# A bitwise top-k threshold search: its per-bit comparison on GpSimd instead of VectorE, and a larger background share

## Chip, cores, metric

One core of a Trainium2 chip. The metric is the device time of one execution in microseconds (us); the median of three runs is given. PE is TensorE's matmul, PEld its weight load, DVE is VectorE, ACT is ScalarE, POOL is GpSimd, SP is the queue that issues most DMAs.

## What is computed

One layer of an encoder on x of 2048 tokens by 1024 channels, float32. A projection gives queries, a latent key and value, indexer queries and keys, pool inputs and gates. An indexer scores every admissible key for each query; the 256 best keys are kept, and 8 heads attend to these alone. A pooling mixer and two sigmoid gates, an output projection, a layer norm and a convolutional feed-forward follow. Of the reference, only this bears on the change:

```python
idx_score = jnp.einsum('bqh,bqhs->bqs', wib.astype(jnp.float32) * head_w_scale, rel)
idx_score = jnp.where(admissible[None], idx_score, -jnp.inf)
_, sel = lax.top_k(idx_score, topk)
```

## The kernel before

The tokens are cut into 16 blocks of 128 queries, and four groups of four blocks. The main stream of work is, in order: projection of the indexer columns (`proj_index`, four groups); then for each group the pool columns, the queries and the gates (`proj_pool`, `proj_q`, `proj_gates`); then attention over 32 units (a unit is one group and one head), the mixing of the branches (`mix_out`), and the feed-forward. Every matmul is three float32r matmuls on split operands, and the main stream is written so that TensorE always has the next one.

The top-k is found without sorting. For each query, `index_scores` builds the scores, and `select` builds a threshold F bit by bit, from bit 31 down to 0. In each bit, a block's scores are counted against the candidate in F in two pieces: ACT sums the signs of one piece into `ca`, and DVE counts the other piece into `cd`. The blocks go in three background jobs (`GROUPS`): blocks 2 to 7, 8 to 11 and 12 to 15 (blocks 0 and 1 need no selection). Each job has two halves of two to four blocks that take turns, so that one half's counts lie beside the other half's decision. `decide` is that decision: is 2 cd - ca below a limit, and so which candidate is next. There are 32 bits, 3 jobs and 2 halves, so 192 decisions. At the end of a job each block is finished: counts against the found threshold, signs (`sg`), a mask of equals, a running count along the row (`tensor_tensor_scan`, one DVE instruction of up to 2048 elements), and the mask `m`, stored to DRAM.

What sets the order of the work: the selection is a Python generator in the list `bg`. `turn` (L461 and after) runs after every step of the main stream. It adds `RATE` times the modelled TensorE time to a credit (at most `CAP`, 1.5 us), and pulls background steps while the credit is positive and the modelled backlog of DVE and ACT is under 3 us. A step costs the larger of its modelled DVE and ACT time (`Paced` has the model; POOL's time isn't charged). So `RATE` and the cost of a step set how far the selection has come at any point of the main stream.

The other thing that pulls the generator is `load_mask` (L1191 and after). It is called in the attention when a block's mask is to be loaded, and if that block isn't finished yet, it runs the rest of the job at once:

```python
while self.selected < b:
    if next(self.bg[0][1], "end") == "end":
        self.bg.pop(0)
```

All engine instructions are recorded by a wrapper (`Paced`, L133), so the trace names that line for all; tiles tell them apart. `g`, `h` and `F` are the tiles of a decision, `cd` and `ca` its two sums, `mx` a score tile's row extreme in the attention. Each engine runs its instructions in the order in which they stand.

Of the kernel before, what the change touches and what calls it, by code (L numbers as in the profile page):

```python
# [15 lines left out]
OP = mybir.AluOpType  # L16
# [52 lines left out]
FINE = "fine"  # L69
PAUSE = "pause"  # L70
GRAIN = 1
RATE = 0.75
CAP = 1.5
EARLY = 2
SWITCH = "A--"
# [270 lines left out]
class Kern:  # L346
# [83 lines left out]
    def turn(self, step=None):  # L430
# [8 lines left out]
        pe, work = self.clocks.pe, self.clocks.work  # L439
        self.credit = min(self.credit + RATE * (pe - self.seen), CAP)  # L440
        self.seen = pe
# [632 lines left out]
    def select(self, halves):  # L1074
# [6 lines left out]
        nc = self.nc  # L1081
# [13 lines left out]
        def decide(k, bit):  # L1095
            cd, ca = acc[k]
            nh = len(halves[k])
            g_ = self.sml([P, 4], tag="g")[:, :nh]
            h = self.sml([P, 4], I32, tag="h")[:, :nh]
            f2 = self.sml([P, 4], I32, tag="F")[:, :nh]  # L1100
            lim = 2.0 * TOPK - 1.0 - ws[k]
            nc.vector.scalar_tensor_tensor(g_, cd, 2.0, ca, op0=OP.mult, op1=OP.subtract)
            yield
            if bit == 31:
                nc.vector.tensor_scalar(h, g_, lim, -1.0, op0=OP.is_lt, op1=OP.mult)
                yield
                nc.vector.tensor_scalar(f2, h, 0x40000000, None, op0=OP.bitwise_xor)
            else:
                nc.vector.tensor_scalar(h, g_, lim, float(2 ** bit), op0=OP.is_lt, op1=OP.mult)
                yield  # L1110
                nc.vector.scalar_tensor_tensor(f2, h, 2 ** (bit - 1) if bit else 0, F[k],
                                               op0=OP.bitwise_xor, op1=OP.bitwise_xor)
            F[k] = f2

        pend = None
        for bit in range(31, -1, -1):
            for k, half in enumerate(halves):
                f = F[k].bitcast(F32)
                w, nh = ws[k], len(half)
                cd, ca = self.sml([P, 4], tag="cd")[:, :nh], self.sml([P, 4], tag="ca")[:, :nh]  # L1120
                for i, b in enumerate(half):
                    ja, jd = self.M([P, 1024], BF16), self.M([P, 1024], BF16)
                    nc.scalar.activation(ja[:, :w], back[b], AF.Sign, bias=f[:, i:i + 1], scale=-1.0,
                                         accum_out=ca[:, i:i + 1])
                    n = front[b].shape[1]
                    nc.vector.tensor_scalar(jd[:, :n], front[b], f[:, i:i + 1], None, op0=OP.is_ge, op1=OP.add,
                                            accum_out=cd[:, i:i + 1])
                    if pend:
                        next(pend, None)
                    yield  # L1130
                if pend:
                    for _ in pend:
                        pass
                acc[k] = (cd, ca)
                pend = decide(k, bit)
        for _ in pend:
            pass
        for k, half in enumerate(halves):
# [21 lines left out]
            for i, b in enumerate(half):  # L1160
# [9 lines left out]
                                               op0=OP.mult, op1=OP.subtract)  # L1170
# [953 lines left out]
```

## Time and profile before

| | |
|---|---|
| three runs | 3159.14, 3161.13, 3167.12 us (median 3161.13) |
| the profiled execution | 3160.95 us; span from first to last instruction 3159.2 us |
| mean granted TensorE clock | 0.989 of full speed |
| PE busy | 3041.4 us (96%) |
| PEld busy | 2536.1 us (80%) |
| DVE busy | 2445.5 us (77%) |
| ACT busy | 1613.7 us (51%) |
| POOL busy | 541.5 us (17%) |

How to read it: an engine that is busy for 96% of the span leaves 118 us in which it waits. A change to work on other engines can at most give back such waits, and what a lower granted clock adds around them; the place of each wait in time says which work it hangs on. A busy DVE or ACT costs nothing by itself.

### The profile page before, as it was taken

To read this page: it belongs to the slowest core of one execution; us is meant where nothing else is said; L and a number is where in the kernel's file an instruction comes from. 1 tells how busy PE (TensorE), PEld (TensorE's weight loads), DVE (VectorE), ACT (ScalarE), POOL (GpSimd) and SP (SyncE) were. 2 spreads that over 40 slices of the span, in tenths; PEclk is the share of its full clock that TensorE was granted. 3 is DMA by queue.
4 is the path that set the end of the run, shared out by engine and by line. 5 is a ranking of instruction groups with operands and counts; after the bars stand their busy time and mean duration, and the time that the engine had idled before them with its cause. 6 is when DMAs were issued, how large, how long until landed. Compare 5 with 4: busy or idle time off the path is not lost. (4 is left out here: it accounts for less than half of the span.)

```text
span 3159.2 us, 43928 instructions
## 1 busy us (share of the span) xinstructions
PE 3041.4 (96%) x14750; PEld 2536.1 (80%) x14750; DVE 2445.5 (77%) x4563; ACT 1613.7 (51%) x3085; POOL 541.5 (17%) x528
## 2 busy tenths in 40 slices
PE   8999899999999999979999999999999999999998
PEld 8887688888888788768787778887778888888887
DVE  5588887987699899888776688999886655656676
ACT  3468846874578787657611144444442222433253
POOL 2002010010020221100231234554411111100011
PEclk9999899999999999989999999999999999999999
DMA  7668783755466332221264778887888866998753
GB/s 255 242 208 298 262 336 138 275 213 184 145 256 250 102 104 84 70 80 62 82 225 162 262 259 303 299 296 284 289 305 321 313 214 224 366 397 328 262 199 110
DMA packets 325872, 715.88 MB, mean 227 GB/s; under 512 B 27466, under 2 KB 132366, under 8 KB 325646
## 3 DMA queue, kind: packets, MB, share of 16 engines
q1 hardware_dynamic: 317006, 697.34, 62.0%
q10 hardware_dynamic: 8640, 15.73, 1.3%
q8 instruction: 117, 1.92, 0.3%
q14 instruction: 109, 0.89, 0.1%
HBM read 454.85 MB, written 258.11 MB: 226 GB/s over the span
## 5 line engine op out<-in xcount | busy, mean ns | idle before, releaser
L133 PE MATMUL p<-b,b 128*128 128x512 f32 (+3 forms) x12568 | 2824.0, 381 | 71.3 <-DVE b L133 25.9
L133 PEld LDWEIGHTS p<-b,b 128*128 128x128 f32 x12568 | 2255.5, 190 | 511.0 <-DVE b L133 32.9
L133 DVE TENSOR_TENSOR b<-p,b 128x512 f32<-128x512 f32 (+3 forms) x622 | 390.6, 654 | 144.6 <-PE p L133 97.8
L133 ACT ACTIVATE b<-p 128x512 fp32r<-128x512 f32 (+11 forms) x634 | 360.6, 604 | 259.1 <-PE p L133 244.0
L133 ACT ACTIVATE b<-b 128x512 fp32r<-128x512 f32 (+3 forms) x344 | 270.5, 805 | 323.2 <-DVE b L133 143.4
L133 DVE TENSOR_TENSOR b<-b,b 128x1024 fp32r<-128x1024 f32 (+6 forms) x302 | 340.0, 1136 | 87.5 <-ACT b L133 38.0
L133 ACT ACTIVATE m<-b,F 128x448 bf16<-128x448 f32 (+3 forms) x448 | 366.2, 820 | 52.8 <-DVE F L133 40.3
L133 DVE TENSOR_SCALAR_CACHE_REDUCE m<-b,F 128x512 bf16<-128x512 f32 (+6 forms) x476 | 372.5, 808 | 7.3 <-DMA gm<-m 3.8
L133 ACT ACTIVATE b<-m 128x512 fp32r<-128x512 f32 x215 | 133.3, 628 | 345.0 <-DVE m L133 133.7
L133 DVE SCALAR_TENSOR_TENSOR b<-b,cw,b 128x1023 f32<-128x1023 f32 (+1 forms) x176 | 246.2, 1411 | 69.7 <-ACT b L133 68.7
L133 ACT ACTIVATE b<-b,cw 128x1024 f32<-128x1024 f32 x88 | 106.9, 1236 | 269.5 <-DVE b L133 260.5
L133 POOL TENSOR_TENSOR b<-b,b 128x1024 f32<-128x1024 f32 (+3 forms) x62 | 148.8, 2402 | 490.2 <-DVE b L133 289.4
L133 PE MATMUL p<-ident,b 128*128 128x128 f32 x1248 | 199.0, 278 | 17.0 <-DVE b L133 8.9
L133 ACT ACTIVATE b<-b,mx 128x1024 f32<-128x1024 f32 (+2 forms) x192 | 171.6, 896 | 70.5 <-DVE mx L133 68.1
L133 PEld LDWEIGHTS p<-ident,b 128*128 128x128 f32 x1248 | 154.3, 142 | 53.1 <-DVE b L133 13.1
L133 DVE TENSOR_TENSOR b<-m,b 128x512 fp32r<-128x512 f32 x215 | 155.6, 732 | 53.1 <-ACT b L133 52.9
L133 DVE SCALAR_TENSOR_TENSOR b<-b,ws,b 128x768 f32<-128x768 f32 (+5 forms) x154 | 154.0, 1025 | 42.2 <-ACT b L133 39.3
L133 DVE CUSTOM_DVE_ANT_0 b<-p,b 128x1024 f32<-128x1024 f32 (+7 forms) x128 | 125.6, 984 | 39.1 <-PE p L133 30.9
L133 PE MATMUL p<-kst,b 128*128 128x384 f32 (+3 forms) x656 | 147.8, 358 | 2.8 <-ACT b L133 2.0
L133 ACT ACTIVATE m<-p 128x512 f32<-128x512 f32 (+2 forms) x172 | 100.8, 586 | 74.6 <-PE p L133 67.9
L133 PEld LDWEIGHTS p<-kst,b 128*128 128x128 f32 x656 | 111.0, 188 | 23.1 <-ACT b L133 12.4
L133 DVE TENSOR_TENSOR b<-p,m 128x512 f32<-128x512 f32 x132 | 89.7, 682 | 10.8 <-PE p L133 10.7
(126 smaller groups left out, 1528.4 us busy)
## 6 DMA issues: line engine op xcount, KB each, us to landing
b<-wk SPq DMA_DIRECT2D x339, 512.0 KB
wk<-b SPq DMA_DIRECT2D x211, 512.0 KB
b<-h SPq DMA_DIRECT2D x88, 512.0 KB
b<-in_w_ffn_up_dram SPq DMA_DIRECT2D x44, 512.0 KB
h<-b SPq DMA_DIRECT2D x44, 512.0 KB
b<-vv SPq DMA_DIRECT2D x80, 256.0 KB
hs<-b SPq DMA_DIRECT2D x33, 512.0 KB
b<-hs SPq DMA_DIRECT2D x33, 512.0 KB
```

The costliest lines, as they stand in the source:

```text
L133: return f(*args, **kw)
```

## The change

```diff
-RATE = 0.75
+RATE = 0.8
...
-            nc.vector.scalar_tensor_tensor(g_, cd, 2.0, ca, op0=OP.mult, op1=OP.subtract)
+            nc.gpsimd.tensor_scalar(g_, cd, 2.0, -lim, op0=OP.mult, op1=OP.add)
+            nc.gpsimd.tensor_tensor(g_, g_, ca, op=OP.subtract)
+            nc.gpsimd.tensor_scalar(h, g_, 0.0, float(2 ** bit) if bit < 31 else -1.0, op0=OP.is_lt, op1=OP.mult)
             yield
             if bit == 31:
-                nc.vector.tensor_scalar(h, g_, lim, -1.0, op0=OP.is_lt, op1=OP.mult)
-                yield
                 nc.vector.tensor_scalar(f2, h, 0x40000000, None, op0=OP.bitwise_xor)
             else:
-                nc.vector.tensor_scalar(h, g_, lim, float(2 ** bit), op0=OP.is_lt, op1=OP.mult)
-                yield
                 nc.vector.scalar_tensor_tensor(f2, h, 2 ** (bit - 1) if bit else 0, F[k],
                                                op0=OP.bitwise_xor, op1=OP.bitwise_xor)
```

The comparison of a decision, two DVE instructions (g and h), becomes three POOL instructions on the same small tiles. The next candidate F stays on DVE. A decision is emitted in two pieces instead of three. The rate at which the background gets credit goes from 0.75 to 0.80.

What this moves is seen in the order of the built programs (rows as listed; a long scan along a row prints as SCALAR_TENSOR_TENSOR there, and the attention's score reductions as ISA).

First place, DVE in the third job (blocks 12 to 15), late in its bits. Before, two halves' counts and one decision:

```order
L133 TENSOR_SCALAR m_11324,cd_11321<-b_10000,F_11283 128x896
L133 TENSOR_SCALAR m_11338,cd_11321<-b_10235,F_11283 128x1024
L133 TENSOR_SCALAR m_11352,cd_11349<-b_9546,F_11329 128x768
L133 SCALAR_TENSOR_TENSOR g_11355<-cd_11321,ca_11322 128x2
L133 TENSOR_SCALAR h_11356<-g_11355 128x2
L133 SCALAR_TENSOR_TENSOR F_11357<-h_11356,F_11283 128x2
```

The same kind of place on DVE after the change:

```order
L133 TENSOR_SCALAR m_11155,cd_11152<-b_9964,F_11128 128x896
L133 SCALAR_TENSOR_TENSOR F_11160<-h_11159,F_11090 128x2
L133 TENSOR_SCALAR m_11172,cd_11152<-b_10199,F_11128 128x1024
L133 SCALAR_TENSOR_TENSOR F_11196<-h_11195,F_11128 128x2
L133 TENSOR_SCALAR m_11191,cd_11188<-b_9537,F_11160 128x768
```

And on POOL, the two decisions whose F stand in the fence above:

```order
L133 TENSOR_SCALAR g_11158<-cd_11120 128x2
L133 TENSOR_TENSOR g_11158<-g_11158,ca_11121 128x2
L133 TENSOR_SCALAR h_11159<-g_11158 128x2
L133 TENSOR_SCALAR g_11194<-cd_11152 128x2
L133 TENSOR_TENSOR g_11194<-g_11194,ca_11153 128x2
L133 TENSOR_SCALAR h_11195<-g_11194 128x2
```

DVE loses g and h. F now stands behind one count of the other half (F_11160) or, as F_11196 does, directly behind the last count of its own half, and takes h from POOL.

Second place, DVE in the attention, the finishing of block 14 (tiles of 1920 elements). Before, it stands as one run:

```order
L133 TENSOR_SCALAR b_16109<-b_16108 128x1920
L133 TENSOR_TENSOR m_16175<-p_4852_15930,m_16176 64x512
L133 SCALAR_TENSOR_TENSOR b_16110<-b_16109 128x1920
L133 SCALAR_TENSOR_TENSOR nd_16115<-b_16110,fx_16094,cg_16093 128x1
L133 TENSOR_SCALAR nd_16115<-nd_16115 128x1
L133 TENSOR_SCALAR b_16109<-b_16110,nd_16115 128x1920
L133 TENSOR_TENSOR b_16108<-b_16108,b_16109 128x1920
L133 TENSOR_SCALAR b_16120<-b_16108 128x1920
```

After the change, the same instructions begin as follows:

```order
L133 TENSOR_SCALAR b_14800<-b_14799 128x1920
L133 SCALAR_TENSOR_TENSOR b_14801<-b_14800 128x1920
L133 TENSOR_TENSOR b_14847<-p_4533_14842,b_14847 128x512
L133 SCALAR_TENSOR_TENSOR nd_14839<-b_14801,fx_14785,cg_14784 128x1
L133 TENSOR_TENSOR b_14857<-p_4535_14852,b_14857 128x512
L133 TENSOR_SCALAR nd_14839<-nd_14839 128x1
L133 ISA b_14866,mx_14827<-p_4537_14862,b_14584,mx_14827 128x256
```

Block 14's scan now stands ahead of the place where block 12's stood, with the attention's own work between its steps; block 15's (2048 elements) stands shortly behind that place, and block 13's at the start of the attention. Block 12 is finished before the attention, between the last gates. The whole job has ended when the first of the masks 12 to 15 is asked for, so the loop in `load_mask` finds nothing left to run; in the program before, it ran the remainder of block 14 (its second half's counts among it) and all of block 15.

## Rows read from the trace of the kernel before

**Rows 1.** Windows: from:to, length; busy us (count) by engine; clock, DMA share, GB/s.

```profile
1300.00:1400.00 100.00, 75.71 (x389) 62.59 (x389) 81.70 (x150) 56.01 (x110) 10.12 (x13) 0.86 0.24 80
```

**Rows 2.** Timeline of PE, 1300 to 1400 us: start, us, instruction, [idle before, releaser].

```profile
1321.49 0.44 PE L133 MATMUL p<-ident,b 128*128 128x128 f32 x2 [2.75 <-DVE b L133]
...
1324.65 3.25 PE L133 MATMUL p<-b,b 128*128 128x384 f32 x7 [1.13 <-ACT b L133]
...
1350.11 2.19 PE L133 MATMUL p<-b,b 128*128 128x512 f32 x6 [4.16 <-DVE mx L133]
...
1357.77 0.66 PE L133 MATMUL p<-ident,b 128*128 128x128 f32 x4 [1.45 <-DVE m L133]
1366.06 5.82 PE L133 MATMUL p<-b,b 128*128 128x512 f32 x14 [7.63 <-DVE mx L133]
...
1380.97 2.93 PE L133 MATMUL p<-b,b 128*128 128x512 f32 x6 [7.06 <-DVE mx L133]
```

**Rows 3.** Timeline of DVE, 1340 to 1400 us.

```profile
1357.64 4.14 DVE L133 TENSOR_TENSOR_SCAN b<-b 128x1920 f16<-128x1920 f16 x1
...
1364.78 1.22 DVE L133 CUSTOM_DVE_ANT_0 b<-p,b 128x1024 f32<-128x1024 f32 x1
...
1372.13 4.42 DVE L133 TENSOR_TENSOR_SCAN b<-b 128x2048 f16<-128x2048 f16 x1
```

**Rows 4.** Windows of 10 us around the last two blocks and the two before.

```profile
1260.00:1270.00 10.00, 6.73 (x37) 5.37 (x37) 9.72 (x18) 3.54 (x8) 5.75 (x4) 0.95 0.21 63
1270.00:1280.00 10.00, 10.00 (x56) 8.83 (x56) 8.56 (x17) 8.05 (x20) 0.00 (x0) 0.88 0.00 0
...
1320.00:1330.00 10.00, 7.26 (x27) 5.72 (x28) 8.11 (x20) 4.98 (x12) 2.28 (x2) 0.68 0.00 0
...
1350.00:1360.00 10.00, 6.87 (x33) 5.76 (x33) 5.49 (x10) 6.30 (x11) 2.13 (x2) 0.83 0.00 0
1360.00:1370.00 10.00, 3.94 (x9) 3.14 (x10) 8.57 (x13) 1.83 (x3) 0.00 (x0) 0.56 0.26 86
1370.00:1380.00 10.00, 3.90 (x19) 3.00 (x17) 8.39 (x8) 3.05 (x6) 0.00 (x0) 0.84 0.04 14
1380.00:1390.00 10.00, 9.03 (x39) 7.42 (x40) 7.61 (x14) 4.72 (x8) 1.42 (x2) 0.74 0.69 228
```

**Rows 5.** Timeline of all engines, 1258 to 1272 us, block 12.

```profile
1263.46 4.00 DVE L133 TENSOR_TENSOR_SCAN b<-b 128x1664 f16<-128x1664 f16 x1
1264.06 4.45 POOL L133 TENSOR_TENSOR b<-m,b 128x512 fp32r<-128x512 f32 x1
...
1267.95 0.66 PE L133 MATMUL p<-ident,b 128*128 128x128 f32 x4 [3.13 <-DVE b L133]
```

**Rows 6.** Tiles g and F on DVE: count, duration ns min/median/max, first and last start.

```profile
L133 DVE SCALAR_TENSOR_TENSOR g<-cd,ca x192: 89/157/864, 187.0 to 1213.0; 128x2 f32<-128x2 f32 x160, 128x4 f32<-128x4 f32 x32
L133 DVE TENSOR_SCALAR h<-g x192: 151/169/898, 187.1 to 1222.1; 128x2 int32<-128x2 f32 x160, 128x4 int32<-128x4 f32 x32
...
L133 DVE TENSOR_SCALAR_CACHE_REDUCE m<-b,F x476: 332/868/1283, 186.0 to 1346.0; 128x128 bf16<-128x128 f32 x33, 128x320 bf16<-128x320 f32 x33, 128x768 bf16<-128x768 f32 x23, 128x640 bf16<-128x640 f32 x23
```

**Rows 7.** Timeline of POOL in the branch mixing: small operations of 128x1.

```profile
1627.71 1.31 POOL L133 TENSOR_SCALAR lv<-mv 128x1 f32<-128x1 f32 x1 [2.25 <-DVE mv L133]
...
1629.76 0.19 POOL L133 TENSOR_TENSOR lt<-lr 128x1 f32<-128x1 f32 x1
1630.03 0.19 POOL L133 TENSOR_TENSOR lt<-lt,lv 128x1 f32<-128x1 f32 x1
```

**Rows 8.** Windows: the stretch of the index scores and gates, and the projections after.

```profile
190.00:420.00 230.00, 209.98 (x945) 171.71 (x946) 195.83 (x698) 182.06 (x480) 19.25 (x29) 0.96 0.83 291
420.00:1060.00 640.00, 637.54 (x2914) 528.46 (x2912) 540.53 (x1225) 422.58 (x755) 50.72 (x71) 1.00 0.58 209
```

**Rows 9.** Timeline of PE, 180 to 420 us: its two longest waits there.

```profile
331.49 1.65 PE L133 MATMUL p<-b,wpool 128*128 128x512 f32 x3 [7.34 <-ACT m L133]
336.73 1.65 PE L133 MATMUL p<-b,wpool 128*128 128x512 f32 x3 [3.59 <-ACT m L133]
```

## Prediction

> **What bounds the kernel now.** I read the windows first, to find where TensorE waits at all; then its waits in the one stretch that stood out; then the engine that they name. From 420 to 1060 us, the projections under which most of the selection runs, PE is busy 637.5 of 640 us at full clock [rows 8]: there, work taken off DVE or put on POOL is worth nothing as long as PE goes on being fed. The stretch that stands out is 1300 to 1400 us: PE busy 75.7 of 100, granted clock 0.86 [rows 1]. Its six waits add up to 24.2 us, and the long ones name DVE's `mx`, a score reduction that came late [rows 2]. DVE isn't idle then. From 1357.64 it runs the finishing of block 14, and the next score reduction starts only at 1364.78; block 15's scan follows at 1372.13 [rows 3]. This is the forced run: the masks of blocks 14 and 15 were asked for before their job had ended, `load_mask` pulled the rest of it into DVE's queue in one piece, and the attention's reductions stood behind it. The reader should see two things: the kernel is bound by PE, and the selection costs time only where its steps stand ahead of something that PE needs at once.
>
> **What the waits cost.** A wait costs its own time and a lower granted clock beside it. For the second I take, in a 10 us window, PE's busy time times what the clock lacks [rows 4]. The forced run: waits of 4.16, 1.45, 7.63 and 7.06, together 20.3; clock from 1350 to 1390, 1.2 + 1.7 + 0.6 + 2.3 = 5.9; total 26.2 us [rows 2, 4]. Block 13's scan, which came as an ordinary step: waits of 2.75 and 1.13, clock 2.3 in 1320 to 1330; total 6.2 [rows 2, 4]. Block 12's, also ordinary: one wait of 3.13 behind a scan of 4.00 [rows 5], clock 0.3 + 1.2 [rows 4]; total 4.7. Together 37.0 us hang on the finishing of these four blocks.
>
> **The rate and the cheaper decision.** Both put the selection ahead of where it was: 6.7% more credit per us of TensorE, and two DVE operations fewer in each decision's cost. The order shows the result: the job has ended before mask 12 is asked for, so the forced run goes, and all 37.0 us go with their places. What comes back: block 15's scan stands about where block 12's did and gets its price, 4.7. Block 14's stands somewhat earlier, in the same kind of work; between 4.7 and 6.2, I take 5.4. Block 13's now stands at the start of the attention, among short score tiles; nothing there shows a scan, so it lies between 0 and 6.2, and I take 4.7, the price of the nearest row. Block 12 is finished between the last gates, where PE has whole products in hand, as it had when PE lost 2.5 us in 640 [rows 8]; between 0 and 4.7, I take 2. That is 16.8 us back, and 20.2 gained.
>
> **The decision on POOL.** 192 decisions lose g (157 ns) and h (169 ns) on DVE [rows 6]: 62.6 us of DVE time, at no point the path itself. They gain three POOL operations. Small dependent ones start 0.27 us apart and take 0.19 [rows 7], so 0.27 + 0.27 + 0.19 = 0.73 from the sums to h; the crossings from DVE to POOL and back aren't in these rows, and I give them one more step: 1.0 us as an estimate. POOL has room: 576 times 0.19 is 109 us more, in 870 us of which it used 70 [rows 8]. What matters is who waits. F stands in DVE's queue, and all of DVE waits with it: the splits of the next weights, the other half's counts, and through F also ACT's counts, with the gates' evictions queued behind them. What stands on DVE between a half's last count and its F is the cover. By the order, 42 of the 192 have nothing there, 41 under 0.5 us, and 109 more than that, mostly one count of the other half (0.33 to 1.28 us, median 0.87 [rows 6]). With 1.0 us each, the uncovered rest adds up to 82 us, against 62.6 saved: DVE gets later by some 19 us between 190 and 1060, where it has 133.7 us idle [rows 8]. So this lies beside other work almost everywhere. The exception is 190 to 420, where DVE is busy 195.8 of 230 and PE already waits 20 us [rows 8]. Bounds: nothing, if cover and idle time take it all (or 10.9 gained, see below), and 19 lost, if all of it reaches PE. I take 2, about the share that PE waits in that stretch.
>
> POOL operations can also be held up by DVE. In rows 5 a POOL operation that began during DVE's scan took 4.45 us and ended only after the scan; in rows 7 the first small operation, behind the layer norm's large two-input DVE operation, took 1.31 us where its like take 0.19. The Trainium skill ("SBUF — State Buffer", Who interferes with whom) says why: a DVE instruction with two SBUF inputs and a GpSimd instruction that reads SBUF exclude each other for the whole instruction. These rows agree, and the rule speaks against this change: the split of every weight is such a DVE instruction. By it the sum is that of rival (b).
>
> **Sum.** -37.0 + 16.8 + 2 = -18.2 us. The profiled execution took 3160.95 us, 0.2 below the median of the three runs, so about 3143.
>
> **Rivals.** A difference under 0.3%, some 9.5 us, can't be told from none here; 3151.6 to 3170.6 counts as the same.
> (a) The scans cost as much as in the forced run wherever they stand. Its two blocks cost 26.2 us for both, of which the counts' 4.16 would not recur: 11 each. Three in the attention give 33 back, and with 2 for the decisions the gain shrinks to 2: 3159, the same. For it: DVE was busy 7.6 to 9.7 of 10 us in six of these seven windows [rows 4], and block 15's scan is longer than block 12's, 4.42 against 4.00 [rows 3, 5]. Against: blocks 12 and 13, as ordinary steps, cost half of that, and the order has score reductions between a block's steps.
> (b) Slower: the lock. If each decision's POOL chain meets one large DVE operation, it takes 1.0 + 1.31 - 0.19 = 2.1 us [rows 7]. The same count over the order then gives 276 us uncovered; less 62.6 saved and 133.7 of idle time, 80 reach PE: 3161 - 20 + 80 = 3221. It decides from a chain of about 1.8 us on (226 us uncovered: what is saved, the idle time, the 20 us gained and the 9.5). Less would do if little of that idle time can be used. Against it: while DVE's operation holds POOL up, DVE is at work and not waiting, and the counts, which read one tensor, stand next to most decisions.
> (c) Better: the two waits of 7.34 and 3.59 us at 331 and 336 [rows 9] name ACT. There the gates' evictions stand behind counts that wait for F. If a DVE relieved of g and h brings F earlier, these 10.9 us go, and with them about half of what the clock lacks in that stretch (210 times 0.04 [rows 8], so 4): 3143 - 2 - 15 = 3126. Against it: POOL's chain makes F later, not earlier, where nothing covers it.
> That the job doesn't end earlier, and nothing moves, is excluded by the order.
>
> **How the numbers follow.** The forecast's mechanism gets 0.58: the forced run is one clear place, its end is in the order, and the bounds of its returns, 9.4 to 21.8 us, with 0 to 5 for the decisions, leave 3133 to 3151. (c) gets 0.12, (a) 0.20, (b) 0.10. Faster by over 0.3% is the forecast and (c), 0.70; the same is (a), 0.20; slower is (b), 0.10. The range reaches from (c) to (a): 3126 to 3158.
>
> **What would show it.** Right: in 1300 to 1400 PE is busy over 95 of 100 at a clock near 1.0; no wait on `mx` over 4 us; the last `F` count on DVE lies before 1220 us instead of at 1346 [rows 6]; scans of 1664 to 2048 elements stand apart, with waits of 2 to 4 us each; g and h on POOL take about 0.19 us and start 0.27 apart. Wrong: DVE's waits for h add up to far over 82 us (b); 190 to 420 is more than 5 us longer than now; or the waits behind the scans of blocks 13 to 15 are 7 us each (a).

## The result, and the profile after

| | before | after |
|---|---|---|
| median of the runs | 3161.13 us | 3177.28 us (3176.17 to 3187.75, five runs) |
| ratio to before | | 1.0059, 95% interval 1.0047 to 1.0071 |
| profiled execution; span | 3160.95; 3159.2 us | 3177.28; 3175.5 us |
| mean granted clock | 0.989 | 0.986 |
| DVE busy / POOL busy | 2445.5 / 541.5 us | 2388.9 / 661.1 us |

The change makes the kernel 16 us slower; 18 us faster was forecast. Three marks in time show where it went. The attention writes `rinv` once for each unit on DVE, the first 16 times with a RECIPROCAL and then with a TENSOR_TENSOR ahead of it. The view of this tile gives the first and the last start of each kind. Before:

```profile
L133 DVE RECIPROCAL rinv<-ssum x16: 157/172/178, 1066.9 to 1190.5; 128x4 f32<-128x4 f32 x16
L133 DVE TENSOR_TENSOR rinv<-ssum x16: 150/159/496, 1207.8 to 1556.8; 128x4 f32<-128x4 f32 x16
```

After:

```profile
L133 DVE RECIPROCAL rinv<-ssum x16: 165/170/179, 1101.8 to 1235.0; 128x4 f32<-128x4 f32 x16
L133 DVE TENSOR_TENSOR rinv<-ssum x16: 151/160/1080, 1251.4 to 1571.9; 128x4 f32<-128x4 f32 x16
```

Up to the first mark lie the projections and the start of the attention: 1101.8 against 1066.9, so 34.9 us lost. Between the first and the 16th: 133.2 against 123.6, 9.6 lost. From there to the last: 336.9 against 366.3, 29.4 gained. Together 15.1 us later at 1571.9, and the rest of the program adds one more.

**What came as forecast.** The windows that answer to [rows 1] and [rows 8]:

```profile
1300.00:1400.00 100.00, 94.74 (x545) 80.35 (x546) 85.63 (x171) 73.24 (x151) 11.72 (x16) 0.97 0.31 102
...
190.00:420.00 230.00, 201.97 (x902) 162.44 (x901) 172.72 (x550) 177.61 (x471) 60.99 (x210) 0.94 0.79 269
420.00:1060.00 640.00, 627.38 (x2838) 518.34 (x2837) 507.83 (x1013) 431.61 (x780) 129.00 (x443) 0.99 0.60 215
```

The forced run is gone: PE is busy 94.7 of 100 us in 1300 to 1400, where it was 75.7. But 190 to 420 has lost 8 us of PE's busy time and 420 to 1060 another 10, at a lower clock in both, although DVE has 23 and 33 us less to do there than in [rows 8]. In PE's timeline the longest waits of these stretches stand at the pool mapping, which takes `wpool` once in each of the four groups, and, like the two of [rows 9], they name ACT's `m`, the sigmoid that empties a gate's product and so gives its buffer back:

```profile
337.40 1.22 PE L133 MATMUL p<-b,wpool 128*128 128x512 f32 x2 [5.17 <-ACT m L133]
345.65 0.80 PE L133 MATMUL p<-b,wpool 128*128 128x512 f32 x1 [6.60 <-ACT m L133]
590.89 1.22 PE L133 MATMUL p<-b,wpool 128*128 128x512 f32 x2 [5.89 <-ACT m L133]
1014.75 1.25 PE L133 MATMUL p<-b,wpool 128*128 128x512 f32 x3 [3.76 <-ACT m L133]
```

The first two answer to the two of [rows 9]; in the second and fourth group the kernel before had no wait of this kind. Its fourth mapping is one row:

```profile
981.72 2.96 PE L133 MATMUL p<-b,wpool 128*128 128x512 f32 x12
```

The mappings are a part of the loss alone; the section on where the share costs divides it. Block 13's scan, at the start of the attention, shows on DVE and on PE:

```profile
1105.01 3.89 DVE L133 TENSOR_TENSOR_SCAN b<-b 128x1792 f16<-128x1792 f16 x1
1108.82 0.67 DVE L133 CUSTOM_DVE_ANT_0 b<-p,b 128x512 f32<-128x512 f32 x1
```

```profile
1109.55 0.62 PE L133 MATMUL p<-b,b 128*128 128x256 f32 x3 [3.96 <-DVE mx L133]
```

**The decision.** The count of one half and its F on DVE, with the three POOL operations between them:

```profile
577.64 1.01 DVE L133 TENSOR_SCALAR_CACHE_REDUCE m<-b,F 128x768 bf16<-128x768 f32 x1
578.57 0.08 DVE L133 DVE_READ_ACCUMULATOR m<-b,F 128x1 f32 x1
579.57 0.16 DVE L133 SCALAR_TENSOR_TENSOR F<-h,F 128x2 int32<-128x2 int32 x1 [0.91 <-POOL h L133]
```

```profile
578.74 0.19 POOL L133 TENSOR_SCALAR g<-cd 128x2 f32<-128x2 f32 x1 [1.21 <-DVE m L133]
579.01 0.19 POOL L133 TENSOR_TENSOR g<-g,ca 128x2 f32<-128x2 f32 x1
579.30 0.24 POOL L133 TENSOR_SCALAR h<-g 128x2 int32<-128x2 f32 x1
```

The chain has the length that was estimated: the count ends at 578.65, F starts at 579.57, 0.92 us later; each crossing between the engines is under 0.1. In the kernel before, with g and h on DVE, the same way takes 0.31 us (579.48 to 579.79). DVE waits for `h` 123 times, 87.4 us in total (82 were forecast); the whole view of that wait is with the experiments on the chain below.

### The profile page after: what moved, and what is told of

Same layout as the page of the kernel before. It is cut to its first block, busy times and chain, and to the rows that moved or that the text cites. A ratio compares the mean times of both kernels' runs of the same rounds, so it can differ in the third digit from the quotient of the medians.

```text
span 3175.5 us, 44227 instructions
## 1 busy us (share of the span) xinstructions
PE 3049.6 (96%) x14750; PEld 2541.0 (80%) x14750; DVE 2388.9 (75%) x4179; ACT 1617.6 (51%) x3085; POOL 661.1 (21%) x1104
## 5 line engine op out<-in xcount | busy, mean ns | idle before, releaser
L133 ACT ACTIVATE m<-b,F 128x448 bf16<-128x448 f32 (+3 forms) x448 | 365.9, 820 | 60.7 <-DVE F L133 46.3
L133 POOL TENSOR_SCALAR g<-cd 128x2 f32<-128x2 f32 x192 | 44.8, 233 | 733.4 <-DVE m L133 679.2
L133 PEld LDWEIGHTS p<-kst,b 128*128 128x128 f32 x656 | 111.9, 189 | 26.2 <-ACT b L133 12.9
```

Of the source, the lines that this page charges most:

```text
L133: return f(*args, **kw)
```

## Experiments: share and decision apart

The first theory was that POOL's chain explains all of it; its rival, that the share does, whoever decides. Each run is timed against the kernel before on the same chip, whose median was 3160.7 us with the first four kernels (share, POOL alone, one step, longer chain), 3162.1 with the next four (shorter chain, last job, first jobs, 0.85) and 3159.3 with the rest. The columns "lost" are the differences of the three stretches above to the kernel before, from the run's own `rinv` rows (one profiled execution, so some us off the median). Behind the last `rinv`, where nothing was changed, these executions scatter between 1599.9 and 1607.3 us; so the three columns needn't add up to the difference of the medians.

| run | median, us | ratio (95% interval) | lost to 1st `rinv` | 1st to 16th | 16th to last |
|---|---|---|---|---|---|
| after | 3177.3 | 1.0059 (1.0047 to 1.0071) | 34.9 | 9.6 | -29.4 |
| share alone | 3167.9 | 1.0026 (1.0016 to 1.0035) | 29.3 | 9.3 | -29.4 |
| POOL alone | 3172.5 | 1.0037 (1.0024 to 1.0051) | 9.6 | 0.2 | -3.2 |
| DVE, one step | 3164.4 | 1.0015 (1.0006 to 1.0024) | 24.9 | 10.0 | -29.5 |
| longer chain | 3232.7 | 1.0228 (1.0214 to 1.0242) | 87.1 | 10.7 | -29.1 |
| shorter chain | 3157.8 | 0.9991 (0.9982 to 1.0000) | 18.8 | 9.8 | -29.6 |
| more POOL work | 3178.1 | 1.0060 (1.0048 to 1.0073) | 33.0 | 10.0 | -29.9 |

**The share alone** (kernel before):

```diff
-RATE = 0.75
+RATE = 0.8
```

> The kernel before with the share at 0.80 and nothing else: g and h stay on DVE. By its order the job has ended before mask 12 is asked for, as in the changed kernel. Theory 1 (the decision on POOL delays F, and with it DVE and ACT, and the projections pay some 46 us for it): without POOL the loss before 1300 us stays away and the gain of the vanished forced run is kept, 3161 - 37 + 17 = 3141, between 3130 and 3150. Theory 2 (the denser placement of the selection's steps, by the share, is what makes ACT late in the projections, whoever takes the decision): the first unit of the last half is reached as late as in the changed kernel, 3170 to 3185.

Measured: 3167.9 us, between the two forecasts, so neither theory holds as it stood. The forced run's gain is all there (-29.4), and 38.6 us are lost ahead of it with no POOL operation added.

**POOL alone** (changed kernel, `RATE = 0.75`):

> The changed kernel with the share back at 0.75: the decision on POOL alone. By its order blocks 14 and 15 are again finished in one piece in the attention (31 DVE operations). Theory 1 (the POOL chain is what costs): the loss of some 46 us before 1300 is still there and the forced run's 26 us are not given back, 3195 to 3210. Theory 2 (the share's placement costs): the projections are as in the kernel before, 3155 to 3168.

Measured: 3172.5, again between the two. The decision on POOL costs 9.6 us up to the first `rinv`, and the forced run stays.

**The decision on DVE, in one step** (changed kernel):

```diff
-            nc.gpsimd.tensor_scalar(g_, cd, 2.0, -lim, op0=OP.mult, op1=OP.add)
-            nc.gpsimd.tensor_tensor(g_, g_, ca, op=OP.subtract)
-            nc.gpsimd.tensor_scalar(h, g_, 0.0, float(2 ** bit) if bit < 31 else -1.0, op0=OP.is_lt, op1=OP.mult)
+            nc.vector.scalar_tensor_tensor(g_, cd, 2.0, ca, op0=OP.mult, op1=OP.subtract)
+            nc.vector.tensor_scalar(h, g_, lim, float(2 ** bit) if bit < 31 else -1.0, op0=OP.is_lt, op1=OP.mult)
```

> The changed kernel with g and h on DVE again, as the two old operations, issued in one step as the three POOL operations are; share 0.80 and the number of steps as in the changed kernel. Theory 1 (the POOL chain): 3130 to 3150, as the run with the share alone. Theory 2 (placement: one step fewer in each decision, and the share): 3170 to 3185.

Measured: 3164.4, between the two once more. By the order of DVE's rows in the traces, this kernel and the changed one have made the same number of decisions at each pool mapping, and their last four scans stand between the same `rinv`; they differ in who makes g and h: by the medians the decision on POOL costs 12.9 us (13.9 by the ratios). The share and the one step fewer cost the other 3.3. Each part alone makes the kernel slower, the share by 7.2 and POOL by 11.8, and together they cost about the sum.

## Experiments: the chain

**A longer chain** (changed kernel; h is computed three times into the same tile):

> The changed kernel with h computed three times, so two more dependent-in-queue POOL operations of 0.27 us in each decision: the chain grows from about 0.91 to 1.45 us. Theory 1 (waits for the chain reach PE): by the order the uncovered waits grow by some 50 us, and 25 to 50 of it reach the end, 3200 to 3227. Theory 2 (placement): the cover holds, 3174 to 3185. Theory 3 (POOL is held up by DVE's large operations, so that the number of POOL operations counts little): under 10 us more, 3177 to 3187.

Measured: 3232.7, above every band: 55 us for two more operations. They take more than the 0.27 us each that was expected; the three h together take 0.87 us where one takes 0.24:

```profile
591.76 0.87 POOL L133 TENSOR_SCALAR h<-g 128x2 int32<-128x2 f32 x3
```

```profile
592.66 0.16 DVE L133 SCALAR_TENSOR_TENSOR F<-h,F 128x2 int32<-128x2 int32 x1 [0.74 <-POOL h L133]
```

The count of this half ends at 591.11, so the chain is 1.55 us long, 0.63 more than in the changed kernel.

**A shorter chain**: POOL starts from ACT's sum, and two operations instead of three follow DVE's count.

```diff
-            nc.gpsimd.tensor_scalar(g_, cd, 2.0, -lim, op0=OP.mult, op1=OP.add)
-            nc.gpsimd.tensor_tensor(g_, g_, ca, op=OP.subtract)
+            nc.gpsimd.tensor_scalar(g_, ca, 0.5, 0.5 * lim, op0=OP.mult, op1=OP.add)
+            nc.gpsimd.tensor_tensor(g_, cd, g_, op=OP.subtract)
```

> The changed kernel with POOL's first operation on ACT's sum instead of DVE's: half of ca plus half the limit first, then cd minus that, then the comparison. In 157 of 192 decisions POOL waits for DVE's count, so there the chain behind the count is two operations instead of three, 0.64 instead of 0.91 us; by the order the uncovered waits fall from 87 to some 45 us. If DVE's waits for h are what the decision on POOL costs (12.8 us between the changed kernel and the same steps on DVE): 3167 to 3173. If it is POOL's time or the crossing as such, whatever the chain's length: 3175 to 3180.

Measured: 3157.8, 19.5 us less than the changed kernel, and below its own band. Where no other work covers the chain, F starts after a wait of 0.70 us where it had waited 0.91. DVE's waits for `h` fell to 74.8 us in total, not to the 45 that were expected.

**More POOL work outside the chain**: the two operations of the longer chain, into a tile that nobody reads.

```diff
+            for _ in range(2):
+                idle = self.sml([P, 4], I32, tag="hx")[:, :nh]
+                nc.gpsimd.tensor_scalar(idle, g_, 0.0, float(2 ** bit) if bit < 31 else -1.0, op0=OP.is_lt, op1=OP.mult)
```

> The changed kernel with two more POOL operations in each decision, the same two as in the run with the longer chain (3233), but written to a tile that nobody reads, behind h: POOL has the same work, the chain from the count to F has three operations as in the changed kernel, and DVE's and ACT's orders are the changed kernel's. If the chain's length is what costs: 3175 to 3185. If POOL's load costs (its SBUF traffic beside DVE, or its queue, where the gates' and the pools' own operations stand): 3220 to 3235.

Measured: 3178.1, as the changed kernel and as the first expectation has it. POOL's load costs nothing here; the time from the count to F costs. In these kernels, which share their order on DVE and ACT, the waits say the same. Columns: who waited for whom, us in total, times, longest us. First the shorter chain, in DVE's and ACT's views:

```profile
DVE F L133 <- POOL h L133: 74.8, 105, 4.3
...
ACT m L133 <- DVE F L133: 33.8, 34, 3.8
```

the changed kernel:

```profile
DVE F L133 <- POOL h L133: 87.4, 123, 2.6
...
ACT m L133 <- DVE F L133: 46.3, 42, 4.0
```

the longer chain:

```profile
DVE F L133 <- POOL h L133: 161.3, 177, 2.7
...
ACT m L133 <- DVE F L133: 115.4, 106, 4.7
```

and, of the run with more POOL work, ACT's row alone:

```profile
ACT m L133 <- DVE F L133: 44.4, 41, 4.0
```

A late F stops ACT too: its counts (`m<-b,F`) stand ahead of the gates' sigmoids in ACT's order. (The sums don't rank kernels with another order: ACT's is 58.4 us with the share alone, whose time is shorter than the changed kernel's.) Per us of chain: 0.21 us less, over 192 decisions, is 40 us, and 19.5 of them came back; 0.63 us more is 121 us, and 55 of them reached the end. About half of what the chain gains or loses arrives at the end.

## Experiments: where the share costs

**The last job alone gets the higher share** (kernel before):

```diff
+LAST = 0.9
...
-        self.credit = min(self.credit + RATE * (pe - self.seen), CAP)
+        rate = RATE if len(self.bg) > 1 else LAST
+        self.credit = min(self.credit + rate * (pe - self.seen), CAP)
```

> The kernel before, decisions on DVE, share 0.75 for the first two selection jobs as before and 0.90 for the last one (blocks 12 to 15). By its order the scans of blocks 12 to 15 are issued at nearly the same places of the attention's matmuls as with the share at 0.80 for all, and nothing is forced. Theory A (a share of 0.80 costs where the first jobs meet the second pool stage, 9 us at 573 to 600 us, and that goes back with 0.75): 3150 to 3160. Theory B (a denser last job costs more in the third gates and the fourth pool stage than it saves): 3165 to 3180.

**The first jobs alone** (the same lines, 0.80 and `LAST = 0.75`):

> The kernel before, decisions on DVE, share 0.80 for the first two jobs and 0.75 for the last: the counterpart of the run with the faster last job. By its order block 15's last three operations alone are forced. Theory A (the loss at the second pool stage hangs on the first two jobs): it stays, 9 us at 573 to 600, and the run takes 3160 to 3172. Theory B (the denser last job costs): the loss at 1000 to 1030 goes, 3145 to 3158.

**A share of 0.85 for all** (`RATE = 0.85`, kernel before):

> The kernel before with the share at 0.85, decisions on DVE. By its order all four scans of the last job are issued before the attention's first matmul, so neither the forced run nor a scan in the attention is left: of the kernel before's 47 us of waits and lost clock in the attention some 38 go without a return. Theory A (each block's finishing costs PE where it stands in the attention, little under the gates; the share costs 17 us in the projections at 0.80, and more in proportion, 25 to 35, at 0.85): 3148 to 3160. Theory B (the share's cost in the projections doubles again, 50 or more): 3170 to 3190. Theory C (the 17 us at 0.80 are an accident of where a job's steps meet the pool stages and don't grow): 3130 to 3145.

| run | median, us | ratio (95% interval) | lost to 1st `rinv` | 1st to 16th | 16th to last |
|---|---|---|---|---|---|
| 0.75, last job 0.90 | 3172.1 | 1.0029 (1.0019 to 1.0040) | 28.0 | 12.7 | -31.1 |
| 0.80, last job 0.75 | 3169.9 | 1.0024 (1.0016 to 1.0033) | 16.3 | 19.1 | -28.3 |
| 0.85 | 3169.5 | 1.0022 (1.0013 to 1.0031) | 41.7 | 11.2 | -43.6 |
| 0.85, quiet at the mapping | 3174.5 | 1.0046 (1.0033 to 1.0059) | 33.0 | 9.7 | -29.9 |
| shorter chain, 0.75 | 3160.3 | 1.0002 (0.9993 to 1.0011) | 0.8 | 0.7 | -2.4 |
| shorter chain, 0.85, quiet | 3162.0 | 1.0006 (0.9997 to 1.0015) | 27.3 | 3.6 | -32.0 |

PE issues the same matmuls up to each mapping in all these kernels. The first `wpool` matmuls of the three mappings that matter start at 322.44, 564.46 and 981.72 in the kernel before, at 331.31, 573.55 and 998.13 with the share alone, and the starts and ends of the mappings divide what is lost up to the first `rinv`:

| run | to 1st mapping | in it | to 2nd | in it | to 4th | in it | to 1st `rinv` |
|---|---|---|---|---|---|---|---|
| after | 7.4 | 1.5 | 9.4 | 6.7 | 2.0 | 4.3 | 3.6 |
| share alone | 8.9 | -1.0 | 1.2 | 5.8 | 1.5 | 4.8 | 8.1 |
| POOL alone | 2.9 | -1.2 | 3.5 | 0.0 | 3.4 | 0.0 | 0.9 |
| DVE, one step | 6.1 | 0.3 | 2.7 | 5.9 | 2.4 | 2.7 | 5.0 |
| shorter chain | 4.5 | -0.6 | 8.0 | 5.7 | 0.8 | 0.1 | 0.2 |

So the mappings hold 9.6 of the share's 29.3 us. Ahead of the first one PE waits 1.5 us more, and most of the 8.9 is a lower granted clock (0.97 against 0.99 in the kernel before); a part of it is scatter, since the three other runs whose first jobs have 0.75 lie between -0.1 and 4.1 there. The 8.1 at the end hold block 12's finishing. The selection needs to be only a little further: by the order on DVE, 35, 71 and 162 decisions have been made when the first, second and fourth mapping starts at 0.75, and 37, 75 and 172 at 0.80. At the third, the second job is over at either share (128), and PE waits in none.

The places moved with the job that had the share: the wait at the second pool mapping (580 us) is gone with 0.75 in the first jobs and there with 0.80, the one at the fourth (1000 us) goes with 0.75 in the last. The times didn't follow: with the faster last job theory A's 3150 to 3160 was missed and theory B's band hit (three waits of 2.8, 5.0 and 3.7 us came at the fourth mapping, then 7.5 and 6.6 at the attention's start); the faster first jobs ended in theory A's band; 0.85 missed all three bands, B's by half a us, gains 43.6 us in the attention and pays 52.9 for it. All four shares cost 7 to 10 us.

**No selection step near the pool mapping**, share 0.85:

```diff
...
-        while self.bg and self.clocks.backlog() < SLACK and self.credit > 0:
+        while self.bg and not self.quiet and self.clocks.backlog() < SLACK and self.credit > 0:
...
                 yield from self.pool_map(g)
+                self.quiet = False
...
                 ps = self.PS1()
+                self.quiet = j == 2 and i == 1 or self.quiet
                 yield from self.proj_t(ps, w, i * P)
...
```

> The share alone (decisions on DVE), at 0.85, and no selection step is issued from the third pair of gates' second product to the end of the pool mapping, once in each of the four groups. By its order the job ends at the same matmul, and the last four scans stand at the same places, as with the share of 0.80 alone (3168). Theory A (in the projections PE waits because ACT's counts stand ahead of the gates' evictions when the pool mapping claims PSUM buffers): the waits on ACT's m at 331 to 345, 581 and 1004 shrink from 10, 5 and 4 us to under 2 each, with the clock beside them 15 to 30 us in all: 3138 to 3155. Theory B (the waits come with the selection's density and return elsewhere in the gates): 3160 to 3175.

Measured: 3174.5, in theory B's band. At the first two mappings the waits are shorter than at 0.80 (5.5 against 9.9 us, 4.4 against 5.0), but no shorter than at 0.85 without these lines (4.7 and 3.0), and at the fourth there are two, of 2.1 and 4.4 us, against one of 4.7. Theory A, that the steps issued just ahead of the mapping are to blame, fell. The traces show a lag that is older. 28 us at the fourth mapping, up to its start in the kernel before, over its wait with the share alone, then with the shorter chain at 0.80 (windows, columns as in [rows 1]):

```profile
954.00:982.00 28.00, 28.00 (x126) 23.16 (x125) 26.79 (x73) 24.52 (x46) 0.00 (x0) 1.00 0.86 316
```

```profile
977.00:1005.00 28.00, 24.12 (x105) 19.62 (x105) 26.79 (x73) 26.07 (x49) 0.00 (x0) 0.95 0.80 302
```

```profile
973.00:1001.00 28.00, 28.00 (x125) 23.19 (x124) 24.44 (x53) 24.68 (x47) 6.63 (x32) 1.00 0.83 307
```

DVE has no wait in either of the first two: 26.79 of 28 us busy, the rest being the gaps between small operations. (From 970 to 998, up to the mapping with the share alone, DVE is busy 26.74 us, and PE still all 28.) It has no reserve at either share. From one count of block 12 on DVE to the next, one bit (four counts on each engine) takes 5.40 us in both where nothing else stands between, while PE ends a gate's product every 5.44 us (24 matmuls, 0.227 us apart). What differs is how many of ACT's counts stand between two sigmoids in this stretch: with 0.75 between 3 and 4 (28 in the last eight gaps), with 0.80 nearly always 4. With 0.75, ACT has caught up with PE and waits for it, and the last sigmoid ahead of the mapping starts 0.2 us behind the mapping's first matmul; in ACT's timeline, the sigmoids:

```profile
976.54 0.60 ACT L133 ACTIVATE m<-p 128x512 f32<-128x512 f32 x1 [0.59 <-PE p L133]
...
981.92 0.60 ACT L133 ACTIVATE m<-p 128x512 f32<-128x512 f32 x1 [1.60 <-PE p L133]
```

With the share alone, ACT waits for F, the last sigmoid comes at 1003.64, 5.5 us behind the mapping's first matmul, and PE, which needs its buffer, stands:

```profile
998.74 1.04 ACT L133 ACTIVATE m<-b,F 128x896 bf16<-128x896 f32 x1 [0.43 <-DVE F L133]
...
1003.64 0.58 ACT L133 ACTIVATE m<-p 128x512 f32<-128x512 f32 x1
```

```profile
998.13 2.26 PE L133 MATMUL p<-b,wpool 128*128 128x512 f32 x9
1004.27 1.65 PE L133 MATMUL p<-b,wpool 128*128 128x512 f32 x3 [3.88 <-ACT m L133]
```

So at 0.80 nearly a whole bit is queued for each product, and DVE's 5.40 us for the bit leave next to nothing of PE's 5.44 for the product. A lag that came with earlier bits isn't made up (three of the four bits between 57 and 31 us ahead of this mapping took 6.6 to 7.0 us, as other DVE work stands between the counts there). ACT falls behind through F, over several products, and the first place where PE needs buffers in quick succession shows it. That reading agrees with the other runs: one bit takes 5.25 us here with the shorter chain, and the wait is gone at the same share; it takes 5.50 in the changed kernel, more than a product, where the chain has replaced g and h. At the second mapping the shorter chain still has a wait, of 4.9 us.

**The shorter chain with the share of 0.75**, and **the shorter chain with the quiet mapping at 0.85**:

> The decision on POOL with the chain of two behind DVE's count, share 0.75. Theory A (chain and share add up: the chain of two is worth 7 us against DVE's decision in the same steps, the share of 0.75 another 4 to 7 against 0.80): 3149 to 3157. Theory B (what the two-operation chain gains comes from where the steps fall at 0.80): 3160 to 3170.

> Both edits together: the decision on POOL with the chain of two, and no selection step around the pool mapping, share 0.85. Theory A (both costs are separate): 15 to 25 us below the chain of two alone (3158), 3130 to 3145. Theory B (the density of the steps costs wherever they stand): 3152 to 3165.

Measured: 3160.3 and 3162.0, both in theory B's bands, and neither told apart from the kernel before. The shorter chain gives at either share (12.2 us at 0.75, 19.5 at 0.80), and the forced run is worth no more than its removal costs. The fastest version is the shorter chain at 0.80: clearly ahead of the changed kernel, and against the kernel before a ratio of 0.9991 whose interval ends at 1.0000. No version here beats the kernel before by what a measurement can tell.

## Why the prediction was wrong

- **The forced run: right.** Its removal with what comes back behind it (-37.0 + 4.7 + 5.4 = -26.9) answers to the last stretch, which measured -29.4 in the changed kernel, -29.4 with the share alone, -29.5 with the decision on DVE. That also answers rival (a): 37.0 less 29.4 leaves 7.6 us for blocks 14 and 15 together, not 11 for each.
- **Blocks 12 and 13: undersized.** For both together 6.7 us were taken, between 0 and 10.9. The stretch from the first `rinv` to the 16th measured 9.6, and block 12's price lies ahead of the first, since its scan starts at 1082.81 and block 13's at 1105.01. With the share alone 8.1 us are lost from the fourth mapping to the first `rinv`, where 2 were taken for block 12; one wait of 5.11 us stands there, at 1086.97, behind its finishing.
- **The denser selection under the projections: the step that failed.** It was costed at nothing, with the argument of [rows 8]: PE busy 637.5 of 640 us, DVE idle for 133.7. The share alone lost 29.3 us up to the first `rinv`, of which 21.2 up to the end of the fourth pool mapping. The idle time is an average. In the last 28 us ahead of that mapping DVE has none even in the kernel before, and PE is full only because ACT still keeps up.
- **The decision on POOL: right mechanism, mis-sized.** Chain (0.92 us measured, 1.0 estimated) and DVE's waits (87.4, 82 estimated) were right, and the 12.9 us lie inside the bounds of 0 to 19. The value taken, 2, was the lateness times the share of time in which PE waits; of the lateness measured, 87.4 less 62.6 = 24.8 us, about half arrived. The range then took 0 to 5 for this term and not its own bounds.
- **Rival (b)** had the right sign for a wrong reason. Of the 576 operations on POOL only 18 took over 0.4 us, 10.9 us more than 0.2 each, and two more operations in each decision, behind the chain, cost nothing. Its threshold, a chain of 1.8 us, was far too high for the same reason as above: 1.55 us gave 3232.7. The Trainium skill ("SBUF — State Buffer", Who interferes with whom) says that a DVE instruction with two SBUF inputs contends with a GpSimd instruction that reads SBUF. The trace agrees: the operations of 1.1 us at 242.36 and 874.13 lie beside DVE operations with two inputs. But they are too few to decide.
- **Rival (c)**: the waits at 331 and 336 didn't go, they became 5.17 and 6.60.

What stays open: how much of the lower clock ahead of the first mapping comes with the share, since each run has one trace. That DVE's 5.40 us for a bit leave no room under PE's 5.44 for a product is read from the traces and from the shorter chain, at the fourth mapping; a run that moves counts from DVE to ACT at 0.80, which would test it by itself, wasn't made.

## What to carry to other kernels

When work moves to a faster schedule "under" a full engine, don't take the helpers' idle time from an average: look at the stretch just ahead of each place where the full engine needs several buffers in a row, and see which helper waits there and which has no gap left. A small decision in a loop of dependent steps is priced by its latency times the number of steps, of which a good part arrives, and not by the busy time it frees; start the chain from the operand that is ready first. Clearing one visible stall by issuing the same work earlier pays only if the earlier place has a free engine.

## What the runs showed of the hardware

Three dependent POOL operations on 128x2 tiles take 0.80 us (starts 0.27 to 0.29 apart, 0.19 to 0.24 each), and the crossings from DVE to POOL and back are under 0.1 us each: 0.92 us from a count to F, where two DVE operations need 0.31. So such steps can stand on POOL where nothing waits for them: 384 more outside the chain (3178.1 against 3177.3 us) left DVE's and ACT's waits as they were (89.9 and 44.4 us for h and F, against 87.4 and 46.3).
